# Keys turned two heads at a time, propagators in one stretch, memory rows two blocks a step: a hybrid decoder step on one Trainium2 core

## The chip, the core and the metric

The kernel runs on one core of a Trainium2 chip. The core has a matrix engine (PE; its weight loads are listed apart as PEld), a vector engine (DVE), a scalar engine (ACT), a general engine (POOL) and a queue engine (SP) that mainly issues transfers. Transfers of all queues share sixteen DMA engines. The large memory is HBM; on the core are SBUF (128 partitions) and PSUM, into which PE writes. The metric is the device time of one execution in microseconds, lower is better. Several runs are taken and their median is compared.

## What is computed

One step of a decoder trunk layer: a prompt of 1024 rows of width 1024, and one new row for each of 8 samples with 1024 cached rows. One input projection feeds three groups of heads. Cut to what matters here:

```
h = rms_norm(x, ln_g);  proj = h @ w_in            # 3480 columns, split by group
# 1. NSA: 8 query heads, 2 key heads of 64; compressed, selected and window branches
k_sel = rope(rms_norm(k, k_norm[1]), pos);  k_win = rope(rms_norm(k, k_norm[2]), pos)
ck, cv = compress(rows);  ck = rope(rms_norm(ck, k_norm[0]), cend)
o_nsa = g_c * attend(q, ck, cv) + g_s * attend(q, selected) + g_w * attend(q, window)
# 2. RWKV-7: 4 heads of 64
S <- S diag(w) + (S (-kk)) (kk a)^T + v k^T;   y = S r
# 3. memory: 4 heads of 64 against 256 memory rows
kv = rms_norm(mem, mem_norm_g) @ w_mem_kv;  o_mem = softmax(q k^T / 8) v
cat = concat(o_nsa * silu(z_nsa), o_rw * silu(z_rw), o_mem * silu(z_mem))
y = x + cat @ w_out
```

The reference's scan over rows of the RWKV group is computed in chunks, with propagators that carry the state over a chunk. Single-precision products are made of parts: an operand is split into a high part `hi` and a low part `lo`, and hi·hi, hi·lo and lo·hi are summed in PSUM.

## The kernel before

It has a phase for the projection and all that it feeds (0 to 497 us in the profile), one for attention, and the output projection (from 797 us on).

**Columns.** The projection runs in blocks of 128 columns of `w_in`. `w_load` (line 268) issues a 512 KB transfer of raw weights on SP's queue into a buffer `wraw`. `w_split` (line 277) makes `whi` on ACT (line 282) and `wlo` on DVE (line 283). `project` multiplies with the transposed rows into tiles `p_pr`: three matmuls for each of eight k, over pieces of 256, 264 and 512 rows (line 306). There are two buffers each for `wraw`, `whi` and `wlo`. The memory's key and value weights, in four blocks of two k (`mem_kv`, lines 1142 to 1147), take the same buffers, in turn with the columns. A buffer for a load comes free when its earlier content was split, one for a split when the earlier matmuls that read it are done.

**The RWKV quarters.** `rwkv_prep` and `rwkv_state` do a quarter of the rows each time, four times. They are generators driven by `drive` (line 597): after a piece of such work that yields n, columns are handed out for n times 1.3 us, so that PE has matmuls while DVE and ACT work on the chain. In `rwkv_state` (lines 932 to 956), for a pair `t` of chunks, `p_g` takes 32 small matmuls, from which DVE makes `PT` (line 945) and `GT` (line 947), each in two instructions of 128x128. A yield of 0.9 lies between the first pair and the second; after the second follow the `p_z` matmuls that read `UV`.

**The ahead stage.** Seventeen of 21 such columns are handed out by `drive`. The four last (columns of `z`, which gates the outputs) alternate with work for the attention:

```
            bg = self.ahead()
            late = self.columns(cols[EARLY:])
            for _ in group(late, 8):
                for _ in islice(bg, BG):
                    pass
```

that is, eight column steps, then eight steps (`BG`) of `ahead`, and so on. `ahead` weaves two generators step by step: one goes through `prompt_cmp` and then `mem_kv`, the other through `attn_keys` for eight blocks of 128 keys and then `q_stack(7)`.

- `attn_keys` (line 1231) loads 128 rows of the normed keys `k_d` into `kd`: four heads (two selected, two window) of 64, in two transfers that write every head twice side by side. Four transposes `p_k` (line 1242) turn each doubled head, so that its 64 dimensions stand on partitions 0 to 63 and again on 64 to 127. ACT makes `kh` (line 1244) and DVE `kl` (line 1245) from it, 128x512.
- `prompt_cmp` turns rows of the compressed branch (`p_xt`, `pxt`), takes them through a small network (`p_hid`, line 1090; `p_co`, line 1104), norms and rotates the result on DVE, copies it on POOL (line 1183) and turns it (`p_k`, line 1190) into `ckh` and `ckl`.
- `mem_kv` (line 1124) turns the memory rows: for each of eight k two transposes `p_mT` (line 1134), `mhi` on ACT and `mlo` on DVE (lines 1137, 1138), one yield a k. Then come the four weight blocks with the matmuls `p_mo` (line 1154).
- `q_stack` turns queries of the last block (`p_q`, line 1307).

The first scores `p_s` (line 83) read `kh` and `kl` and open the attention phase. The order of calls gives the work a priority and the claims of buffers an order; a scheduler then sets the order of instructions on each engine, which is fixed in the program. SP issues its transfers in its own order; one that has to wait holds up those behind it.

Of the kernel before, what the change touches and what calls it, by code (L numbers as in the profile page):

```python
# [10 lines left out]
F32 = mybir.dt.float32  # L11
# [3 lines left out]
AF = mybir.ActivationFunctionType  # L15
OP = mybir.AluOpType
# [10 lines left out]
KB = 2  # L27
# [20 lines left out]
def bc(ap, shape):  # L48
    return ap.to_broadcast(shape)
# [64 lines left out]
class Step:  # L114
# [713 lines left out]
    def rwkv_state(self, Q):  # L828

        nc, PE = self.nc, self.pe  # L830
        V, A, G = nc.vector, nc.scalar, nc.gpsimd
        AM, UV, ar, bk, I = self.AM, self.UV, self.ar, self.bk, self.ident
# [5 lines left out]
        for g, o, p, b in blocks:  # L838
            x = AM[o, 2 * p:2 * p + 2, :, b * 32:b * 32 + 32]
            V.tensor_tensor(x, x, bc(self.eye[o, None, None, :], [32, 2, 4, 32]), op=OP.add)  # L840
            V.tensor_tensor(Tt[o].rearrange("p (t h) e -> p t h e", t=2), x, bc(self.pairs[o, None, None, :], [32, 2, 4, 32]),
                            op=OP.mult)
# [21 lines left out]
        for i in range(1, 5):  # L864
            ps = self.pw.tile([128, 8, 32], F32, name="p_iy", tag="w")
# [7 lines left out]
            elif i < 4:  # L873
                t = i - 2
                pr = self.pw.tile([128, 4, 64], F32, name="p_r", tag="w")
                for h in range(4):
                    for p in range(2):
                        o, k = slice(p * 64, p * 64 + 64), slice(64 - p * 64, 128 - p * 64)
# [4 lines left out]
            ps = self.pw.tile([128, 8, 32], F32, name="p_it", tag="w")  # L883
# [18 lines left out]
        lo, up = [blocks[0][1], blocks[2][1]], [blocks[1][1], blocks[3][1]]  # L902
        Ti = self.Ti
        ps = self.pw.tile([128, 8, 32], F32, name="p_iy", tag="w")
# [7 lines left out]
        ps = self.pw.tile([128, 8, 32], F32, name="p_it", tag="w")  # L912
# [6 lines left out]
        W = [None] * 2  # L919
        for t in range(2):  # L920
            px = self.pw.tile([128, 4, 128], F32, name="p_x", tag="w")
            for h in range(4):
                for p in range(2):
                    o = slice(p * 64, p * 64 + 64)
# [3 lines left out]
            for p in range(2):  # L928
                o = slice(p * 64, p * 64 + 64)
                V.tensor_copy(UV[o, 2 * t + p], px[o, :, 64:128])  # L930
        yield 0.6
        GT, PT = [None] * 2, [None] * 2
        half = [slice(p * 64, p * 64 + 64) for p in range(2)]
        for t in range(2):
            GT[t] = self.rs.tile([128, 2, 2, 64], F32, name="GT", tag=f"GT{t}")
            PT[t] = self.rs.tile([128, 2, 2, 64], F32, name="PT", tag=f"PT{t}")
            pgs = [self.pw.tile([128, 4, 64], F32, name="p_g", tag="w") for _ in range(2)]
            for k in range(2):
                for c in range(2):
                    for h in range(2):  # L940
                        for pg, o, p in zip(pgs, half, range(2)):
                            x = AM[o, 2 * p + t, 2 * c + h, 64:128] if k else bkT[t][o, c, p, h * 64:h * 64 + 64]
                            PE.matmul(pg[half[h], 2 * k + c, :], W[t][o, 2 * c + h, :], x, start=True, stop=True)
            for p, pg in enumerate(pgs):
                V.tensor_tensor(PT[t][:, :, p, :], pg[:, 0:2], bc(self.eye2[:, None, :], [128, 2, 64]), op=OP.add)
            for p, pg in enumerate(pgs):
                V.tensor_tensor(GT[t][:, :, p, :], pg[:, 2:4], ar[:, :, t, 1, p, :], op=OP.add)
            if t == 0:
                yield 0.9
        pz = self.pw.tile([128, 4, 2, 64], F32, name="p_z", tag="w")  # L950
        for n in range(4):
            for c in range(2):
                for h in range(2):
                    PE.matmul(pz[half[h], n, c, :], bkT[n // 2][:, c, n % 2, h * 64:h * 64 + 64], UV[:, n, 2 * c + h, :],
                              start=(n == c == 0), stop=False, skip_group_check=True)
        yield 0.9
        pyy = [self.pw.tile([128, 2, 2, 64], F32, name="p_yy", tag="w") for _ in range(2)]
        for t in range(2):
            for c in range(2):
                for h in range(2):  # L960
                    for p in range(2):
                        PE.matmul(pyy[h][half[1 - p], t, c, :], AM[:, 2 * p + t, 2 * c + h, 64:128], UV[:, 2 * t + p, 2 * c + h, :],
                                  start=(t == c == 0), stop=False, skip_group_check=True)
        Zs = [self.Z]
        for n in range(4):
            Zn = self.rc.tile([128, 2, 64], F32, name="Zn", tag="Z", bufs=5)
            for c in range(2):
                for h in range(2):
                    PE.matmul(pz[half[h], n, c, :], PT[n // 2][half[h], c, n % 2, :], Zs[n][half[h], c, :],
                              start=False, stop=True, skip_group_check=True)  # L970
            V.tensor_tensor(Zn[:], pz[:, n], bc(self.gC[:, :, n:n + 1], [128, 2, 64]), op=OP.mult)
            Zs.append(Zn)
            if n < 3:
                yield 0.8
        self.Z = Zs[4]
        for t in range(2):
            for c in range(2):
                for p, h in ((0, 0), (1, 1), (1, 0), (0, 1)):
                    PE.matmul(pyy[h][half[1 - p], t, c, :], GT[t][half[h], c, p, :], Zs[2 * t + p][half[h], c, :],
                              start=False, stop=(c == 1), skip_group_check=True)  # L980
        ys = []
        for t in range(2):
# [142 lines left out]
    def mem_kv(self):  # L1125
        nc, I, O = self.nc, self.I, self.O
        V, A, PE = nc.vector, nc.scalar, nc.tensor
        xs = self.mem_rows
        his = [self.slot(j, [128, 4, 256], F32R, f"mhi{j}") for j in (4, 0)]
        los = [self.slot(j, [128, 4, 256], F32R, f"mlo{j}") for j in (5, 1)]  # L1130
        for k in range(8):
            ps = self.pM.tile([128, 512], F32, name="p_mT", tag="m")
            for t in range(2):
                PE.transpose(ps[:, t * 128:(t + 1) * 128], xs[t][:, k * 128:(k + 1) * 128], self.ident[:])
            g = self.v("mem_norm_g", k)
            hi, lo = his[k // 4][:, k % 4, :], los[k // 4][:, k % 4, :]
            A.activation(hi, ps[:, :256], AF.Copy, scale=g)
            V.scalar_tensor_tensor(lo, ps[:, :256], g, hi.bitcast(F32), op0=OP.mult, op1=OP.subtract)
            yield
        po = [self.pw.tile([128, 512], F32, name="p_mo", tag="w") for t in range(2)]  # L1140
        for k in range(0, 8, 2):
            raw = self.wr.tile([128, 2, 512], F32, name="wraw")
            nc.sync.dma_start(raw[:], I["w_mem_kv"][0, k * 128:(k + 2) * 128, :].rearrange("(k p) c -> p k c", p=128))
            wh = self.wp.tile([128, 2, 512], F32R, name="whi")
            wl = self.wp.tile([128, 2, 512], F32R, name="wlo")
            A.activation(wh[:], raw[:], AF.Copy)
            V.tensor_tensor(wl[:], raw[:], wh[:].bitcast(F32), op=OP.subtract)
            yield
            for j in range(2):
                for t in range(2):  # L1150
                    cs = slice(t * 128, (t + 1) * 128)
                    h, l = his[k // 4][:, (k + j) % 4, cs], los[k // 4][:, (k + j) % 4, cs]
                    for i, (a, w) in enumerate(((h, wh), (h, wl), (l, wh))):
                        PE.matmul(po[t][:], a, w[:, j], start=(k + j == 0 and i == 0), stop=(k + j == 7 and i == 2))
            yield
        dst = O["mem_kv_prompt"]
        for t in range(2):
            d0 = bass.AP(tensor=dst.tensor, offset=dst.offset + t * 128 * 512, ap=[[512, 128], [1, 512]])
            kv = self.slot(2 + t, [128, 8, 64], F32, f"mkv{t}")
            A.activation(kv[:, 4:8].rearrange("p h d -> p (h d)"), po[t][:, 256:512], AF.Copy)  # L1160
            self.norm_rope(po[t][:, 0:256].rearrange("p (t c) -> p t c", t=1), 5, 1, 4, None, out=kv[:, 0:4])
            nc.sync.dma_start(d0, kv[:].rearrange("p h d -> p (h d)"))
            yield
# [67 lines left out]
    def attn_keys(self, i, tag="m"):  # L1231
        nc = self.nc
        A, G = nc.scalar, nc.gpsimd
        kk = self.kt.tile([128, 4, 2, 64], F32, name="kd4", tag="kd4", bufs=KB)
        for s in range(2):
            nc.sync.dma_start(kk[:, :, s, :], self.k_d[i * 128:(i + 1) * 128, :].rearrange("t (j d) -> t j d", d=64))
        if i % 4 == 0:
            nc.sync.dma_start(self.vs[i // 4][:].rearrange("p k b g d -> p k (b g d)"),
                              self.v_d[i * 128:(i + 4) * 128, :].rearrange("(k p) c -> p k c", p=128))
        ps = self.pM.tile([128, 4, 128], F32, name="p_k4", tag=tag)  # L1240
        for j in range(4):
            nc.tensor.transpose(ps[:, j, :], kk[:, j].rearrange("p s d -> p (s d)"), self.ident[:])
        kh, kl = (x[i // 4][:, :, i % 4 * 128:i % 4 * 128 + 128] for x in (self.kh, self.kl))
        A.activation(kh, ps[:], AF.Copy)
        nc.vector.tensor_tensor(kl, ps[:], kh.bitcast(F32), op=OP.subtract)

    def prompt_cmp(self):
        nc, I, O = self.nc, self.I, self.O
# [1267 lines left out]
```

## Time and profile before

| | |
|---|---|
| Runs | 935.43, 937.71, 943.02 us; median 937.71 |
| Profiled execution | 936.7 us, of which the span 934.9 |
| Granted PE clock, mean | 0.998 |
| First scores `p_s` start | 496.62 us |
| PE busy, 425 to 500 us | 70.31 of 75 us |

Times in the profile count from the span's start. A row of groups gives the line, engine, operation and tiles, then the count, the busy time, the mean of one in ns, and the engine's idle time ahead of it with what ended it. In the timeline the columns are start, duration, engine, line and operation, with idle time and its releaser in brackets. Matmuls overlap, so their starts tell more than their durations. A row of a time slice gives each engine's busy time and number of instructions, then the granted clock, the busy share of the DMA engines and GB/s. A row of a tile's view gives the shortest, median and longest duration in ns.

### The profile page before, as it was taken

The page shows a single profiled execution, that of the slowest core. Times are in us where ns is not written, and L with a number is a line of the kernel's source. Part 1 is how long each engine was busy: PE and PEld are TensorE (multiplying, and loading weights), DVE is VectorE, ACT ScalarE, POOL GpSimd, SP SyncE. Part 2 cuts the span into 40 slices and gives each one's busy share as a digit, 9 for nine tenths or more (in the row PEclk, how much of TensorE's full clock was granted, in tenths as well). Part 3 has the DMA queues.
Part 4 walks back from the last instruction along what each step waited for, and adds up shares of the span by engine and source line. Part 5 has one row for each costly group of instructions (what it writes and reads, how often), then busy time and mean ns, then how long its engine had stood idle before and what let it go on. Part 6 is the DMA issues. An engine that isn't in the chain of part 4 may idle for free.

```text
span 934.9 us, 24813 instructions
## 1 busy us (share of the span) xinstructions
PE 899.3 (96%) x9911; PEld 762.7 (82%) x9911; DVE 648.0 (69%) x2013; ACT 434.2 (46%) x987; POOL 178.7 (19%) x270
## 2 busy tenths in 40 slices
PE   8999999999999999999899999999999999999998
PEld 7998888877878788778777788888887887887976
DVE  7668679864777559946457866765678996548454
ACT  7654324232443234213446666666566766424211
POOL 2000000000000000000104444544344765112010
PEclk9999999999999999999999999999999999999999
DMA  8521313241321205524429313432130036986561
GB/s 278 130 78 35 104 41 105 61 115 48 84 86 52 77 19 143 136 65 132 138 85 275 99 56 108 132 108 60 32 87 10 10 113 168 330 249 218 179 239 47
DMA packets 134698, 105.96 MB, mean 113 GB/s; under 512 B 34641, under 2 KB 120600, under 8 KB 134456
## 3 DMA queue, kind: packets, MB, share of 16 engines
q1 hardware_dynamic: 129592, 92.64, 33.8%
q0 software_dynamic: 3200, 10.49, 3.2%
q8 instruction: 78, 1.28, 0.5%
q10 hardware_dynamic: 1792, 1.26, 0.5%
q14 instruction: 36, 0.29, 0.1%
HBM read 85.77 MB, written 22.78 MB: 116 GB/s over the span
## 4 chain that ended last, share of the span: by engine, by line
PE 73%; DVE 17%; ACT 5%; DMA 2%; issue 2%; POOL 0%; SPq 0%; DVEq 0%; ACTq 0%
PE p_pr L86 20%; PE p_out L86 9%; PE p_pr L306 5%; PE p_o L86 5%; PE p_s L86 5%; PE p_pT L86 5%; PE p_hid L86 3%; ACT p L1416 2%; DVE p L1409 2%; PE p_it L86 1%; PE p_iy L86 1%; PE p_sc L86 1%; DVE pt L1377 1%; DVE wlo L283 1%; PE p_tk L86 1%
## 5 line engine op out<-in xcount | busy, mean ns | idle before, releaser
L86 PE MATMUL p_pr<-h,whi 128*128 128x512 f32 (+2 forms) x976 | 237.0, 336 | 2.0 <-DVE zt L318 2.0
L86 PEld LDWEIGHTS p_pr<-h,whi 128*128 128x128 f32 x976 | 158.6, 189 | 19.5 <-issue 2.4
L86 PE MATMUL p_pr<-h,wlo 128*128 128x512 f32 (+2 forms) x488 | 157.6, 326 | 0.6 <-DVE wlo L283 0.6
L1447 POOL TENSOR_SCALAR p<-p,fac,gates 128x640 f32<-128x640 f32 (+7 forms) x128 | 103.3, 817 | 110.9 <-DVE fac L1443 71.1
L1416 ACT ACTIVATE p<-p,nm 128x640 f32<-128x640 f32 (+7 forms) x128 | 93.1, 728 | 56.3 <-DVE nm L1409 51.3
L86 PEld LDWEIGHTS p_pr<-h,wlo 128*128 128x128 f32 x488 | 91.4, 189 | 9.3 <-DVE wlo L283 0.8
L86 PE MATMUL p_pT<-ident,p 128*128 128x128 f32 x528 | 70.8, 279 | 6.9 <-POOL p L1447 1.9
L1075 POOL MEMSET w2d<- 128x128 f32 x1 | 0.2, 204 | 377.2 <-PE p_iy L86 377.2
L86 PEld LDWEIGHTS p_pT<-ident,p 128*128 128x128 f32 x528 | 56.8, 140 | 18.1 <-issue 6.6
L1409 DVE CUSTOM_DVE_ANT_0 p<-p_s,bmask 128x512 f32<-128x512 f32 (+7 forms) x96 | 60.3, 659 | 16.1 <-PE p_s L86 15.4
L306 PE MATMUL p_pr<-h,whi 128*128 128x264 f32 (+2 forms) x320 | 69.3, 310 | 0.0
L86 PE MATMUL p_o<-pt,vs 128*64 128x128 f32 x1056 | 67.9, 276 | 0.4 <-DVE cat L1485 0.4
L283 DVE TENSOR_TENSOR wlo<-wraw,whi 128x1024 fp32r<-128x1024 f32 x33 | 40.3, 1221 | 36.9 <-ACT whi L282 32.6
L86 PE MATMUL p_s<-kh,qs 128*128 128x512 f32 (+3 forms) x191 | 65.2, 354 | 0.2 <-DVE nm L1409 0.2
L282 ACT ACTIVATE whi<-wraw 128x1024 fp32r<-128x1024 f32 x34 | 36.0, 1059 | 59.6 <-PE p_pr L86 47.1
L86 PEld LDWEIGHTS p_o<-pt,vs 128*64 128x64 f32 x1056 | 57.0, 137 | 7.5 <-issue 3.9
L86 PE MATMUL p_s<-kl,qs 128*128 128x512 f32 (+3 forms) x192 | 60.3, 334 | 0.0
L1377 DVE COPY pt<-p_pT 128x512 f32<-128x512 f32 (+1 forms) x72 | 48.2, 673 | 13.2 <-PE p_pT L86 12.4
L306 PEld LDWEIGHTS p_pr<-h,whi 128*128 128x128 f32 x320 | 51.5, 188 | 3.1 <-issue 0.2
L86 PE MATMUL p_out<-woh,chi 128*128 128x512 f32 x128 | 51.7, 404 | 0.0
L86 PE MATMUL p_out<-woh,clo 128*128 128x512 f32 x128 | 50.2, 392 | 0.4 <-DVE clo L2352 0.4
L86 PE MATMUL p_out<-wol,chi 128*128 128x512 f32 x128 | 49.9, 390 | 0.0
(551 smaller groups left out, 1884.3 us busy)
## 6 DMA issues: line engine op xcount, KB each, us to landing
wraw<-in_w_in_dram SPq DMA_DIRECT2D x34, 512.0 KB
pg<-in_c_pool_dram SPq DMA_DIRECT2D x32, 256.0 KB
pg<-in_c_pool_dram SPq DMA_DIRECT2D x48, 128.0 KB
x<-in_x_prompt_dram SPq DMA_DIRECT2D x8, 512.0 KB
z_d<-zt SPq DMA_DIRECT2D x16, 256.0 KB
cat<-z_d SPq DMA_DIRECT2D x8, 512.0 KB
xres<-in_x_prompt_dram POOLq DMA_DIRECT2D x16, 256.0 KB, 3.8
out_dram<-xres POOLq DMA_DIRECT2D x16, 256.0 KB, 3.0
```

Source lines behind the costliest of these rows:

```text
L86: self.last = getattr(self.engine, op)(*a, **k)
L282: nc.scalar.activation(hi[:, :, :n], raw[:, :, :n], AF.Copy)
L283: (low or nc.vector).tensor_tensor(lo[:, :, :n], raw[:, :, :n], hi[:, :, :n].bitcast(F32), op=OP.subtract)
L306: self.last_mm = self.pe.matmul(ps[:m, :b - a], w[:, k, :m], h[k][:, a:b], start=(k == 0 and i == 0), stop=(k == 7 and i == 2))
L1075: nc.gpsimd.memset(w2d[:], 0.0)
L1377: nc.vector.tensor_copy(pt[:, :n], ps[:, :n])
L1409: return V.tensor_tensor_reduce(halves(x), halves(ps), m, -1.0, 3.0e38, op0=OP.add, op1=OP.min, accum_out=nm[:, h, b:b + 1])
L1416: e = A.activation(x, x, AF.Exp, scale=-1.0, bias=nm[:, h, b:b + 1], accum_out=sm[:, h, b:b + 1])
L1447: nc.gpsimd.tensor_scalar(x, x, f[:, h, b:b + 1], gate[:, hd + h, 1 + b:2 + b], op0=OP.mult, op1=OP.mult)
```

## The change

Three edits. Keys: a block is loaded once, 128 rows of 1 KB; a transpose turns two heads at a time, so that heads 0 and 2 land on partitions 0 to 63 and heads 1 and 3 on 64 to 127. ACT and DVE write each half where it belongs in `kh` and `kl` (two instructions of 64x2x128 each). After blocks 3 and 7, four transfers from SBUF to SBUF of 256 KB each fill in the other half. Propagators: `PT` and `GT` of both pairs become one tile each, the `p_g` matmuls of both pairs and `p_z` follow in one stretch, and the two yields of 0.9 become one of 1.6. Memory rows: two k share a PSUM tile and a step, so `mem_kv` has four steps for its transposes instead of eight.

```
-        for t in range(2):
-            GT[t] = self.rs.tile([128, 2, 2, 64], F32, name="GT", tag=f"GT{t}")
-            PT[t] = self.rs.tile([128, 2, 2, 64], F32, name="PT", tag=f"PT{t}")
-            pgs = [self.pw.tile([128, 4, 64], F32, name="p_g", tag="w") for _ in range(2)]
-            for k in range(2):
+        GT = self.rs.tile([128, 2, 2, 2, 64], F32, name="GT", tag="GT")
+        PT = self.rs.tile([128, 2, 2, 2, 64], F32, name="PT", tag="PT")
+        pgs = [self.pw.tile([128, 2, 4, 64], F32, name="p_g", tag="w") for _ in range(2)]
+        for k in range(2):
+            for t in range(2):
                 for c in range(2):
...
-            for p, pg in enumerate(pgs):
-                V.tensor_tensor(PT[t][:, :, p, :], pg[:, 0:2], bc(self.eye2[:, None, :], [128, 2, 64]), op=OP.add)
-            for p, pg in enumerate(pgs):
-                V.tensor_tensor(GT[t][:, :, p, :], pg[:, 2:4], ar[:, :, t, 1, p, :], op=OP.add)
-            if t == 0:
-                yield 0.9
+        for p, pg in enumerate(pgs):
+            V.tensor_tensor(PT[:, :, :, p, :], pg[:, :, 0:2], bc(self.eye2[:, None, None, :], [128, 2, 2, 64]), op=OP.add)
+        for p, pg in enumerate(pgs):
+            V.tensor_tensor(GT[:, :, :, p, :], pg[:, :, 2:4], ar[:, :, :, 1, p, :].rearrange("p c t e -> p t c e"), op=OP.add)
...
-        yield 0.9
+        yield 1.6
...
-        for k in range(8):
-            ps = self.pM.tile([128, 512], F32, name="p_mT", tag="m")
-            for t in range(2):
-                PE.transpose(ps[:, t * 128:(t + 1) * 128], xs[t][:, k * 128:(k + 1) * 128], self.ident[:])
...
+        for k0 in range(0, 8, 2):
+            ps = self.pM.tile([128, 2, 256], F32, name="p_mT", tag="m")
+            for k in (k0, k0 + 1):
+                for t in range(2):
+                    PE.transpose(ps[:, k % 2, t * 128:(t + 1) * 128], xs[t][:, k * 128:(k + 1) * 128], self.ident[:])
...
             yield
...
-        kk = self.kt.tile([128, 4, 2, 64], F32, name="kd4", tag="kd4", bufs=KB)
-        for s in range(2):
-            nc.sync.dma_start(kk[:, :, s, :], self.k_d[i * 128:(i + 1) * 128, :].rearrange("t (j d) -> t j d", d=64))
+        kk = self.kt.tile([128, 2, 128], F32, name="kd4", tag="kd4", bufs=KB)
+        nc.sync.dma_start(kk[:].rearrange("p a b -> p (a b)"), self.k_d[i * 128:(i + 1) * 128, :])
...
-        for j in range(4):
-            nc.tensor.transpose(ps[:, j, :], kk[:, j].rearrange("p s d -> p (s d)"), self.ident[:])
+        for j in range(2):
+            nc.tensor.transpose(ps[:, j, :], kk[:, j], self.ident[:])
...
-        A.activation(kh, ps[:], AF.Copy)
-        nc.vector.tensor_tensor(kl, ps[:], kh.bitcast(F32), op=OP.subtract)
+        half = [slice(0, 64), slice(64, 128)]
+        for g, o in enumerate(half):
+            A.activation(kh[o, g::2], ps[o, 0:2], AF.Copy)
+            nc.vector.tensor_tensor(kl[o, g::2], ps[o, 0:2], kh[o, g::2].bitcast(F32), op=OP.subtract)
+        if i % 4 == 3:
+            for x in (self.kh[i // 4], self.kl[i // 4]):
+                for g in range(2):
+                    nc.sync.dma_start(x[half[1 - g], g::2].bitcast(F32), x[half[g], g::2].bitcast(F32))
```

PE has 16 instructions less (7001 for 7017), DVE 8 less, ACT 8 more; SP's transfers are 559 as before. Three places show what the scheduler makes of it. On PE in the first RWKV quarter, the difference (- before, + after) around the propagators:

```order
 L86 MATMUL p_pr<-h_7_914,whi 128x512
 L86 MATMUL p_pr<-h_7_913,wlo 128x512
-L86 MATMUL p_g<-bkT,W 64x64 x8
-L86 MATMUL p_g<-AM,W 64x64 x8
+L86 MATMUL p_g<-bkT,W 64x64 x16
+L86 MATMUL p_g<-AM,W 64x64 x16
+L86 MATMUL p_z<-UV,bkT 64x64 x16
 L86 MATMUL p_pr<-h_0_245,whi 128x256
```

The second pair's `p_g` and the `p_z` matmuls come forward to the first pair's, and the columns that stood between follow them. On PE in the ahead stage, before, from the compressed branch's output to the memory rows' first transposes:

```order
L1104 MATMUL p_co<-w2d,phid 128x128
L1307 MATMUL p_q<-ident,qhl 128x128 x4
L306 MATMUL p_pr<-h_2_249,whi 128x264
...
L306 MATMUL p_pr<-h_2_811,whi 128x512
L1190 MATMUL p_k<-ident,kd 128x128
L1134 MATMUL p_mT<-ident,mx_6337 128x128
L1134 MATMUL p_mT<-ident,mx_6356 128x128
L306 MATMUL p_pr<-h_2_810,wlo 128x512
```

And after, a little earlier to the same place:

```order
L1240 MATMUL p_k_6524<-ident,kd_6522 128x128 x2
L1279 MATMUL p_xt<-ident,px_6360 128x128 x4
L1240 MATMUL p_k_6539<-ident,kd_6537 128x128 x2
L1087 MATMUL p_hid<-pxt_6483,w1s_6351 128x128 x8
L1311 MATMUL p_q<-ident,qhl 128x128 x4
L1087 MATMUL p_hid<-pxt_6515,w1s_6352 128x128 x8
L1311 MATMUL p_q<-ident,qhl 128x128 x4
L1101 MATMUL p_co<-w2d,phid 128x128
L1311 MATMUL p_q<-ident,qhl 128x128 x4
L1189 MATMUL p_k<-ident,kd 128x128
L1132 MATMUL p_mT<-ident,mx_6305 128x128
```

Before, 26 columns' matmuls stand between `p_co` and the compressed keys' `p_k`, and others further ahead; after, none. On SP's queue, before, the third late column's weights (`wraw` from `w_in`) are asked for right behind the small constants:

```order
L1143 DMA wraw<-in_w_mem_kv_dram 128x2x512
L1040 DMA pe_rows<-in_cmp_pe_dram 32x128
L1067 DMA b1t<-in_cmp_b_dram 64x2x1
L1080 DMA b2b<-in_cmp_b_dram 128x128
L1077 DMA w2d<-in_cmp_w_dram 64x64 x2
L274 DMA wraw<-in_w_in_dram 128x8x128
```

After, the memory's second block stands at that place, and the third column comes behind the eighth key load:

```order
L1234 DMA kd_6490<-k_d 128x256
L1142 DMA wraw<-in_w_mem_kv_dram 128x2x512
L1249 DMA kh_6225<-kh_6225 64x2x512 x2
L1249 DMA kl_6226<-kl_6226 64x2x512 x2
L1234 DMA kd_6506<-k_d 128x256
L1234 DMA kd_6522<-k_d 128x256
L319 DMA z_d<-zt 128x512
L321 DMA z_d<-zt 128x8
L319 DMA z_d<-zt 128x512
L1234 DMA kd_6537<-k_d 128x256
L274 DMA wraw<-in_w_in_dram 128x8x128
```

Here the third memory block and the copies of the first four key blocks also stand ahead of the sixth key load.

More of the change, by code (lines that the diff above doesn't have):

```diff
@@ L931, in rwkv_state @@
         yield 0.6
-        GT, PT = [None] * 2, [None] * 2
         half = [slice(p * 64, p * 64 + 64) for p in range(2)]
-        for t in range(2):
-            GT[t] = self.rs.tile([128, 2, 2, 64], F32, name="GT", tag=f"GT{t}")
-            PT[t] = self.rs.tile([128, 2, 2, 64], F32, name="PT", tag=f"PT{t}")
-            pgs = [self.pw.tile([128, 4, 64], F32, name="p_g", tag="w") for _ in range(2)]
-            for k in range(2):
+        GT = self.rs.tile([128, 2, 2, 2, 64], F32, name="GT", tag="GT")
[3 more added lines that the diff above has]
+            for t in range(2):
                 for c in range(2):
@@ L942, in rwkv_state @@
                             x = AM[o, 2 * p + t, 2 * c + h, 64:128] if k else bkT[t][o, c, p, h * 64:h * 64 + 64]
-                            PE.matmul(pg[half[h], 2 * k + c, :], W[t][o, 2 * c + h, :], x, start=True, stop=True)
-            for p, pg in enumerate(pgs):
-                V.tensor_tensor(PT[t][:, :, p, :], pg[:, 0:2], bc(self.eye2[:, None, :], [128, 2, 64]), op=OP.add)
-            for p, pg in enumerate(pgs):
-                V.tensor_tensor(GT[t][:, :, p, :], pg[:, 2:4], ar[:, :, t, 1, p, :], op=OP.add)
-            if t == 0:
-                yield 0.9
+                            PE.matmul(pg[half[h], t, 2 * k + c, :], W[t][o, 2 * c + h, :], x, start=True, stop=True)
+        for p, pg in enumerate(pgs):
+            V.tensor_tensor(PT[:, :, :, p, :], pg[:, :, 0:2], bc(self.eye2[:, None, None, :], [128, 2, 2, 64]), op=OP.add)
+        for p, pg in enumerate(pgs):
+            V.tensor_tensor(GT[:, :, :, p, :], pg[:, :, 2:4], ar[:, :, :, 1, p, :].rearrange("p c t e -> p t c e"), op=OP.add)
         pz = self.pw.tile([128, 4, 2, 64], F32, name="p_z", tag="w")
@@ L968, in rwkv_state @@
                 for h in range(2):
-                    PE.matmul(pz[half[h], n, c, :], PT[n // 2][half[h], c, n % 2, :], Zs[n][half[h], c, :],
+                    PE.matmul(pz[half[h], n, c, :], PT[half[h], n // 2, c, n % 2, :], Zs[n][half[h], c, :],
                               start=False, stop=True, skip_group_check=True)
@@ L978, in rwkv_state @@
                 for p, h in ((0, 0), (1, 1), (1, 0), (0, 1)):
-                    PE.matmul(pyy[h][half[1 - p], t, c, :], GT[t][half[h], c, p, :], Zs[2 * t + p][half[h], c, :],
+                    PE.matmul(pyy[h][half[1 - p], t, c, :], GT[half[h], t, c, p, :], Zs[2 * t + p][half[h], c, :],
                               start=False, stop=(c == 1), skip_group_check=True)
@@ L1130, in mem_kv @@
         los = [self.slot(j, [128, 4, 256], F32R, f"mlo{j}") for j in (5, 1)]
-        for k in range(8):
-            ps = self.pM.tile([128, 512], F32, name="p_mT", tag="m")
-            for t in range(2):
-                PE.transpose(ps[:, t * 128:(t + 1) * 128], xs[t][:, k * 128:(k + 1) * 128], self.ident[:])
[L1135 to L1138, printed above, removed]
+        for k0 in range(0, 8, 2):
[3 more added lines that the diff above has]
+                    PE.transpose(ps[:, k % 2, t * 128:(t + 1) * 128], xs[t][:, k * 128:(k + 1) * 128], self.ident[:])
+            for k in (k0, k0 + 1):
+                g = self.v("mem_norm_g", k)
+                hi, lo = his[k // 4][:, k % 4, :], los[k // 4][:, k % 4, :]
+                A.activation(hi, ps[:, k % 2], AF.Copy, scale=g)
+                V.scalar_tensor_tensor(lo, ps[:, k % 2], g, hi.bitcast(F32), op0=OP.mult, op1=OP.subtract)
             yield
```

## The prediction, written before the changed kernel ran

> **What bounds the kernel now.** I read the page first: one engine is busy nearly all the time, and the chain that ended last runs mostly through it.
>
> ```profile
> PE 899.3 (96%) x9911; PEld 762.7 (82%) x9911; DVE 648.0 (69%) x2013; ACT 434.2 (46%) x987; POOL 178.7 (19%) x270
> ...
> PE 73%; DVE 17%; ACT 5%; DMA 2%; issue 2%; POOL 0%; SPq 0%; DVEq 0%; ACTq 0%
> ```
>
> So PE's own order sets the time. DVE, ACT and the DMA queue cost only where PE stands still for them. PE takes its instructions strictly in the program's order, so such a standstill can only be filled by matmuls placed at that point of the order. Next I read busy time in slices of 5 us around the key and memory stage. Its last line sums fifteen slices, 425 to 500.
>
> ```profile
> 445.00:450.00 5.00, 3.14 (x20) 2.48 (x18) 0.78 (x2) 2.35 (x4) 0.00 (x0) 1.00 0.56 146
> 450.00:455.00 5.00, 4.38 (x34) 3.75 (x34) 3.06 (x5) 2.70 (x7) 0.00 (x0) 1.00 0.76 189
> 460.00:465.00 5.00, 4.85 (x36) 4.43 (x36) 3.90 (x20) 1.98 (x7) 0.00 (x0) 1.00 0.01 3
> ...
> sum 75.00, PE 70.31 PEld 58.45 DVE 40.50 ACT 28.82 POOL 3.19; mean PE 4.69 PEld 3.90 DVE 2.70 ACT 1.92 POOL 0.21
> ```
>
> PE idles 75.00 - 70.31 = 4.7 us of the 75. The waits of PE in that stretch say for whom:
>
> ```profile
> PE p_k L1242 <- DMA kd<-k_d: 2.4, 2, 1.9
> PE p_mo L1154 <- DVE wlo L1147: 0.5, 1, 0.5
> PE p_k L1190 <- POOL kd L1183: 0.5, 1, 0.5
> ```
>
> Idle time is low because late projection columns (`p_pr`, line 306) stand between the steps of three long chains. The timeline of PE shows it:
>
> ```profile
> 433.85 0.63 PE L1242 MATMUL p_k<-ident,kd 128*128 128x128 f32 x4 [0.59 <-DMA kd<-k_d]
> ...
> 448.44 0.63 PE L1242 MATMUL p_k<-ident,kd 128*128 128x128 f32 x4 [1.86 <-DMA kd<-k_d]
> 448.91 0.60 PE L1275 MATMUL p_xt<-ident,px 128*128 128x128 f32 x4
> ...
> 458.56 0.60 PE L1307 MATMUL p_q<-ident,qhl 128*128 128x128 f32 x4
> 458.91 0.48 PE L306 MATMUL p_pr<-h,whi 128*128 128x256 f32 x2
> ...
> 460.85 0.46 PE L1104 MATMUL p_co<-w2d,phid 128*128 128x128 f32 x2
> 461.14 0.60 PE L1307 MATMUL p_q<-ident,qhl 128*128 128x128 f32 x4
> 461.50 0.49 PE L306 MATMUL p_pr<-h,whi 128*128 128x264 f32 x2
> ...
> 466.31 0.33 PE L1190 MATMUL p_k<-ident,kd 128*128 128x128 f32 x1 [0.49 <-POOL kd L1183]
> ...
> 496.62 0.39 PE L83 MATMUL p_s<-kh,qs 128*128 128x512 f32 x1
> ```
>
> Durations overlap on PE, so I use starts. Four key transposes take 448.91 - 448.44 = 0.47, or 0.117 each. The path from `p_co` to the compressed keys' transpose takes 466.31 - 460.85 = 5.46 us, and PE shows only 0.49 of it as idle: columns fill the rest.
>
> From the first key transpose to the first scores are 62.8 us (433.85 to 496.62). At their start-to-start pitch (0.117 for 128 columns, 0.234 for 512) the instructions there need 53.3 us by my count. The other 9.5 us are 4.1 of idle time (4.7 less the 0.59 ahead of the first row) and 5.4 of handovers: PE goes into a group of transposes and out again about 20 times, 0.27 each.
>
> **Keys, the direct part.** Sixteen transposes go: 16 x 0.117 = -1.9 us, all on PE's path. Each block is now emptied by ACT, DVE, ACT, DVE in turn, on half the partitions but 256 elements each, instead of one ACT and one DVE pass over 512. The nearest rows:
>
> ```profile
> L1244 ACT ACTIVATE kh<-p_k 128x512 fp32r<-128x512 f32 x8 | 4.8, 598 | 10.9 <-PE p_k L1242 10.9
> ...
> L1146 ACT ACTIVATE whi<-wraw 128x1024 fp32r<-128x1024 f32 x4 | 4.2, 1061 | 8.9 <-PE p_pr L306 5.1 <-PE p_mo L1154 3.8
> ...
> L1160 ACT ACTIVATE mkv<-p_mo 128x256 f32<-128x256 f32 x2 | 0.7, 374 | 0.0
> ...
> L1245 DVE TENSOR_TENSOR kl<-p_k,kh 128x512 fp32r<-128x512 f32 x8 | 5.5, 689 | 8.1 <-ACT kh L1244 8.1
> ...
> L382 DVE TENSOR_TENSOR mkv<-p_mo,rq_r 128x256 f32<-128x256 f32 x2 | 0.8, 424 | 0.1
> ```
>
> That is 2 x (0.374 + 0.424) = 1.6 us a block in place of 0.598 + 0.689 = 1.29. With columns between the blocks neither is seen. Where blocks stand next to each other, it is.
>
> **Keys, the transfers.** Sixteen loads become eight, and eight SBUF copies are added, all on SP's queue.
>
> ```profile
> 429.91 1.26 SPq L1236 DMA_DIRECT2D kd<-k_d  x2
> ...
> kd<-k_d SPq DMA_DIRECT2D x16, 128.0 KB
> ```
>
> The issues stay sixteen at about 0.63 us, so SP itself is neither better nor worse off. The first pair was issued by 431.17 and used at 433.85, 2.7 later; one load instead of two may bring it 0.6 earlier, or not at all. I take 0 there. Bytes: 16 x 128 KB become 8 x 128 KB and 8 x 256 KB, one MB more, in a stretch whose DMA engines stand at 0.56 to 0.76. The first four copies (1 MB) and a memory weight block (512 KB) now stand ahead of the sixth and seventh key loads. At the 189 GB/s of the 450 row they take up to 8 us. Most of that passes under fifteen column matmuls (15 x 0.234 = 3.5) and the transposes before. I take 1.2 us of waiting for the sixth load, with bounds 0 and 5. The second four copies land long before 496: 0.
>
> [...] No run here shows such a copy yet.
>
> **Memory rows, and what that moves.** The sixteen transposes, eight ACT and eight DVE passes remain; bundling saves perhaps two handovers. But `mem_kv` yields four times fewer, and steps of `ahead` and column steps alternate in fixed groups. So its first two weight blocks now claim buffers before the third late column, which must wait for the second block's matmuls. The order shows the consequence: the columns that stood between the eighth key block, `p_hid`, `p_co`, the compressed keys and the memory transposes are gone from there, and follow after the memory matmuls. The work is the same, but these chains lose their cover. Chain by chain:
>
> 1. Key blocks six to eight stand back to back with the last two `p_xt`: three emptyings of 1.7 us (1.6 and handoffs) are 5.1, less 14 transposes x 0.117 = 1.6 that run meanwhile: 3.5 us. Lower end 2.0, if ACT runs ahead of DVE; upper end 4.6, if the second weight block's split (1.06 on ACT), queued right ahead of the sixth block's pass, delays that in full.
> 2. Second `p_hid` to `p_co`: 460.85 - 458.56 = 2.29, less one `p_q` of 0.35: 1.9. The first `p_hid` to the second: 0.3.
> 3. `p_co` to the transpose: 5.46, less `p_co` and `p_q` (461.50 - 460.85 = 0.65) and less the column's pass that DVE did in the middle (0.34 between these two starts):
>
> ```profile
> 465.16 0.42 DVE L318 SCALAR_TENSOR_TENSOR zt<-zt,p_pr 128x264 f32<-128x264 f32 x1
> 465.50 0.18 DVE L398 TENSOR_TENSOR nr_o<-nr_o,nr_sq 128x32 f32<-128x32 f32 x1
> ```
>
> That leaves 4.5 us. Nothing else stands there for PE.
> 4. Memory transposes to `p_mo`: 0.5, as the waits of before have for the same matmuls.
>
> New waits: 0.6 for the first load (as before), 1.2, 3.5, 0.3, 1.9, 4.5, 0.5 = 12.5. Handovers: 14 groups in place of 20, 14 x 0.27 = 3.8. Together 16.3 against 4.7 + 5.4 = 10.1 before: +6.2 us.
>
> **Propagators.** Per quarter, both pairs in one stretch: one trip less from columns to 64-wide matmuls and back, and four DVE passes of 256 for eight of 128.
>
> ```profile
> L945 DVE TENSOR_TENSOR PT<-p_g,c_rw x16: 277/282/291, 133.8 to 415.0; 128x128 f32<-128x128 f32 x16
> ...
> 133.87 0.28 PE L86 MATMUL p_pr<-h,wlo 128*128 128x256 f32 x1
> 134.09 0.33 PE L86 MATMUL p_g<-bkT,W 64*64 64x64 f32 x2
> 134.63 0.40 PE L86 MATMUL p_g<-bkT,W 64*64 64x64 f32 x11 [0.22 <-DVE GT L947]
> ...
> 137.74 0.28 PE L86 MATMUL p_pr<-h,wlo 128*128 128x256 f32 x1
> 137.95 1.15 PE L86 MATMUL p_yy<-UV,AM 128*64 128x64 f32 x32
> ```
>
> A trip costs about 0.1 on entry (137.74 to 137.95 is 0.21 where the pitch is 0.117) and as much on leaving: 0.2. The 0.22 wait for `GT` goes once. DVE saves 4 x (2 x 0.28 - 0.424) = 0.5 a quarter, off the path. Sum 4 x 0.2 + 0.2 = -1.0 us. Bounds: -2 (a later wait goes too) to +1.5 (PT and GT of the first pair come later, and a filler step less is handed out).
>
> **Sum.** +6.2 - 1.9 - 1.0 = +3.3 us. After the first scores PE's order is the same, and their inputs do not arrive late, so it is kept to the end. The profiled execution took 936.7 us around its span of 934.9; it lies 1.0 below the median of the runs, 937.71. So 936.7 + 3.3 + 1.0 = 941.0 us.
>
> **Rivals.**
> - *Cover not needed.* Chains shorten where nothing interleaves: load wait 0 (-1.2), key emptying 2.0 (-1.5), handovers counted inside waits (-2.0), propagators at -2 (-1.0). Then 941.0 - 5.7 = 935.3, faster than before. It decides once waits and handovers of the stage stay under 10.1 + 2.9 = 13.0. For it: 5.4 is a remainder, not a row. Against it: items 2 and 3 are durations of chains in the trace, 6.4 us by themselves. Chance 0.20.
> - *The queue.* The copies hold up the sixth to eighth key loads at the upper bound, 5 us: 941.0 + 3.8 = 944.8. For it: the 1.86 wait for a key load at 448.44, behind far less traffic. Chance 0.15.
> - *A cold clock.* A gap of 4.5 us slows PE for a while after. The trace has such a place at the start, after 2.73 us of waiting:
>
> ```profile
> 3.32 5.18 PE L86 MATMUL p_w<-ident 128*128 128x128 f32 x30
> ...
> 10.14 3.62 PE L86 MATMUL p_w<-ident 128*128 128x128 f32 x30
> ```
>
> The same thirty cost 1.6 us more the first time: 941.0 + 1.6 = 942.6. Against it: no wait elsewhere exceeds 2.7, and the clock column reads 1.00 in every slice. Chance 0.10. [...]
>
> **Chances.** The forecast as summed has 0.55; the rivals 0.20, 0.15 and 0.10. From 935.3 to 944.8, widened by a microsecond at either end for the runs' scatter: 934.5 to 946.0. Within 1% (9.4 us, about what a measurement of this kernel can tell from no change) lies nearly all of it: 0.88. Slower by more than that needs the queue and the clock together with the sum, 0.08; faster by more would need the stage's waits gone altogether, 0.04.
>
> **What would show it.** In the profile after: `p_k` of the compressed keys waiting some 4.5 us for POOL or DVE, `p_co` some 2 for DVE, the late key blocks for DVE's `kl`; the first scores at about 500; PE's busy time about 3 us less (1.9 of it transposes). Scores at or before 496.6 would make the forecast wrong; so would key loads that arrive over 3 us after PE is ready for them, or `p_mT` and `p_mo` at half pace.

## The result

The changed kernel took 945.46 us (median of 22 runs, 941.09 to 952.14) against 937.94 for the kernel before (22 runs, 935.43 to 943.02). The ratio is 1.0076, 95% interval 1.006 to 1.0091: by the ratio some 7.1 us slower. The profiled execution took 947.2 us with a span of 945.4, so it is slower than the median run.

| profiled span, us | before | after |
|---|---|---|
| last state matmul `p_yy` of the RWKV quarters starts | 420.6 | 418.9 |
| first scores `p_s` start | 496.6 | 507.4 |
| the stage between | 76.0 | 88.5 |
| from the first scores to the end | 438.3 | 438.0 |

The quarters end 1.7 us earlier, the stage is 12.5 longer, and nothing happens behind it. In the page's view of 40 slices the place is seen at once, in the rows of PE and of its clock:

```profile
PE   8999999999999999898699999999999999999998
...
PEclk9999999999999999999699999999999999999999
```

The 6 in the second row is new: the slice around 460 us. One 5 us slice at a time (the columns as before, the clock right after POOL's count):

```profile
430.00:435.00 5.00, 3.02 (x41) 1.75 (x39) 1.51 (x3) 0.76 (x2) 0.00 (x0) 0.78 0.81 250
435.00:440.00 5.00, 5.00 (x38) 4.98 (x38) 3.58 (x11) 1.69 (x5) 0.00 (x0) 0.88 0.56 168
...
445.00:450.00 5.00, 2.26 (x10) 1.50 (x8) 1.81 (x2) 1.54 (x2) 0.00 (x0) 0.99 0.94 231
450.00:455.00 5.00, 3.37 (x13) 2.20 (x13) 1.79 (x5) 3.01 (x7) 0.72 (x1) 0.50 0.67 190
455.00:460.00 5.00, 5.00 (x23) 4.78 (x24) 1.12 (x3) 1.40 (x5) 0.73 (x1) 0.50 0.52 125
...
465.00:470.00 5.00, 0.76 (x5) 0.75 (x5) 2.98 (x18) 1.31 (x5) 0.41 (x2) 0.69 0.00 0
470.00:475.00 5.00, 5.00 (x22) 4.06 (x21) 2.13 (x5) 2.12 (x6) 0.00 (x0) 0.62 0.00 0
```

Two things go on here: PE waits (2.26, 3.37 and 0.76 us busy out of 5), and three times its clock falls to half: around 434 (0.50 from 434 to 436), from 450 to 460 (0.50), and from 467 to 474 (0.50 from 468 to 472). A slice with a busy PE and a clock of 0.50 looks full and does less: from 455 on, sixteen `p_hid` matmuls take 0.21 us each from start to start, where the kernel before needed 0.12 (rows in the last section). PE's waits of the stage:

```profile
PE p_k L1189 <- POOL kd L1182: 4.2, 1, 4.2
PE p_k L1240 <- DMA kd<-k_d: 2.8, 1, 2.8
PE p_k L1240 <- DMA vs<-v_d: 2.0, 1, 2.0
PE p_co L1101 <- DVE phid L1094: 1.7, 1, 1.7
PE p_k L1240 <- ACT pxt L1281: 1.4, 2, 0.7
PE p_xt L1279 <- DVE kl L1245: 0.2, 1, 0.2
```

They sum to 12.3 us, where the stage before had 4.7. The whole stage in one slice, for the kernel after:

```profile
418.90:507.40 88.50, 76.20 (x455) 64.14 (x449) 44.40 (x158) 30.46 (x71) 3.23 (x6) 0.88 0.43 121
```

and before:

```profile
420.60:496.62 76.02, 71.33 (x468) 59.40 (x463) 41.85 (x149) 29.10 (x63) 3.19 (x6) 1.00 0.44 126
```

PE is busy for 4.9 us more, with 13 matmuls less on record. The clock explains it: summed over 2 us slices, busy time times the missing share of the clock is 8.0 us. This is an estimate, which takes PE to be as slow as its clock; in the trace a `p_mo` matmul of 512 columns took 0.425 us from start to start at 472 us (clock 0.50 to 0.56), one of `p_pr` 0.235 at 445 (clock 1.00), by which it would be an estimated 7.2. With the 8.0, PE's busy time at a full clock would be 76.2 - 8.0 = 68.2, or 3.1 less than before. So in this execution: waits +7.6, work -3.1, clock +8.0, together +12.5; quarters -1.7, the rest -0.3; sum +10.5, as the spans have it (945.4 - 934.9). This is an account of one execution, and its terms are not independent: a slow transpose fills time in which a fast one would leave PE waiting. So a full clock need not have given back all of the 8.0.

The runs agree. Each of the 22 lists its mean granted clock, from 0.982 (952.14 us) to 0.995 (941.09), and a straight line through them falls by 0.7 us for each thousandth, with a correlation of -0.86. Their mean is 0.989. The clocks of the 22 runs of the kernel before are not on record; in the three later comparisons it has 0.996 (31 runs) and 0.995 (26 and 23). By the line through the changed kernel's runs, the difference is worth an estimated 4.3 to 4.7 of the 7.1 us.

### The profile page after: what moved, and what is told of

The parts are those of the page before. It is cut to its first block, busy times and chain, and to the rows that moved or that the text cites. A ratio compares the mean times of both kernels' runs of the same rounds, so it can differ in the third digit from the quotient of the medians.

```text
span 945.4 us, 24777 instructions
## 1 busy us (share of the span) xinstructions
PE 901.8 (95%) x9895; PEld 766.3 (81%) x9895; DVE 648.2 (69%) x2005; ACT 435.4 (46%) x995; POOL 178.6 (19%) x270
## 3 DMA queue, kind: packets, MB, share of 16 engines
q8 instruction: 78, 1.28, 0.5%
## 4 chain that ended last, share of the span: by engine, by line
PE 74%; DVE 15%; ACT 5%; DMA 2%; issue 2%; SPq 1%; POOL 0%; DVEq 0%; ACTq 0%; POOLq 0%
PE p_pr L86 20%; PE p_out L86 9%; PE p_pr L306 7%; PE p_o L86 5%; PE p_s L86 5%; PE p_pT L86 4%; PE p_hid L86 3%; ACT p L1420 3%; DVE p L1413 2%; PE p_it L86 1%; PE p_iy L86 1%; PE p_sc L86 1%; PE p_mo L1153 1%; DVE pt L1381 1%; PE p_tk L86 1%
```

## The experiments

There were three comparisons, each with runs of the kernel before that its kernels share (31, 26 and 23), so ratios are compared, not times. A ratio is not the quotient of the two medians beside it, and can differ from it by 0.0016. The question was first which edit is to blame, then how much is cover and how much the clock.

| run | edit | median, us | before there | ratio, 95% interval | stage, us | PE idle in it |
|---|---|---|---|---|---|---|
| rwkv_alone | propagators only | 935.59 | 936.03 | 1.0001 (0.998 to 1.0022) | 76.6 | 4.8 |
| keys_alone | keys only | 934.69 | 936.03 | 0.9981 (0.9956 to 1.0006) | 74.3 | 4.2 |
| claims_alone | before, four steps fewer | 944.02 | 936.03 | 1.0091 (1.006 to 1.0122) | 83.5 | 10.2 |
| steps_back | after, four steps more | 935.35 | 936.03 | 0.9986 (0.9964 to 1.0008) | 74.3 | 4.2 |
| claims_filled | claims_alone, gap filled | 945.58 | 936.74 | 1.0078 (1.0052 to 1.0103) | 82.3 | 6.5 |
| after_filled | after, gap filled | 943.14 | 936.74 | 1.0073 (1.0044 to 1.0101) | 82.9 | 7.4 |
| copies_elsewhere | after, copies on POOL's queue | 941.84 | 936.74 | 1.0049 (1.003 to 1.0067) | 79.2 | 8.4 |
| six_steps | after, BG = 6 | 930.02 | 936.74 | 0.994 (0.9918 to 0.9961) | 71.0 | 2.2 |
| six_before | before, BG = 6 | 936.93 | 937.75 | 1.0003 (0.9982 to 1.0023) | 73.5 | 3.2 |
| six_no_rwkv | six_steps without propagators | 931.62 | 937.75 | 0.9939 (0.9918 to 0.9961) | 71.0 | 2.5 |
| six_copies_elsewhere | six_steps, copies on POOL's queue | 932.12 | 937.75 | 0.9945 (0.9923 to 0.9966) | 71.9 | 3.1 |

The stage is that of the first table, from one profile each. In all of them the rest behind it is 437.7 to 442.8 us; in the four at 441 and more (keys_alone, claims_filled, copies_elsewhere, six_before) PE was slow there for a while: their longest weight load for `p_s` is 333 or 334 ns, 192 to 195 in the others.

**The propagators alone.** Edit: the hunk of `rwkv_state` on the kernel before.

> The propagator edit alone, on the kernel before. My theory: it gains 1.0 to 1.7 us (the prediction's term was -1.0; the last state matmuls of the changed kernel's profile end 1.7 us earlier than before), so 936.2 to 936.9 against 937.9, clock 0.998, waits of the key stage as before. Rival (the merged stretch makes later steps wait, which eats the gain): 937.9 or more.

The quarters end at 418.8 instead of 420.6, 1.8 earlier, and the first scores come at 495.4 instead of 496.6. Over 12 and 31 runs no gain is left to see: 1.0001, with 0.998 still inside the interval. In the profile 0.6 of the 1.8 comes back in the stage (76.6 instead of 76.0). A reason may be that the shorter yields (1.6 for 1.8) hand out fewer columns in the quarters; no run tests it.

**The keys alone.** Edit: the hunk of `attn_keys` on the kernel before.

> The key edit alone: one load a block, two transposes, copies across partitions; memory rows step as before. My theory: columns still stand in the late chains, so only the 16 transposes count: -1.9 us, 936.0. Rival (the copies on the queue and the longer emptying of a block are what costs): a wait of 2 us or more for a key load stays, and the time is 940 or above.

0.9981 is 1.8 us, the size of the sixteen transposes, though the interval just includes 1. The waits for key loads fall from 2.4 to 1.2 us, all of it at the fourth block, ahead of the copies. Over thirty column matmuls stand between the fifth block and the sixth, and behind the same copies on the same queue PE waits for no key load. So with columns in between, neither the copies nor the longer emptying show as a loss.

**The steps alone.** All instructions of the kernel before, with one line changed:

```
             V.scalar_tensor_tensor(lo, ps[:, :256], g, hi.bitcast(F32), op0=OP.mult, op1=OP.subtract)
-            yield
+            if k % 2:
+                yield
```

> The kernel before with one edit: the memory rows' transposes yield after every second k only, all instructions as before. My theory (fewer steps shift the buffer claims, the third late column comes after the memory matmuls, the chains lose their cover, and PE's clock falls in the gaps): 944 to 947, granted clock below 0.995, PE waits over 4 us for POOL at the compressed keys' transpose. Rival (the loss comes from the keys' transfers): 938 as before.

This is as much as the whole loss: 1.0091, with an interval that holds 1.0076. No key, no propagator and no bundle of memory rows is changed; only where the generator gives way. The waits for the compressed keys and for `p_co` are those of the changed kernel; those for the first and the sixth key load are not there:

```profile
PE p_k L1191 <- POOL kd L1184: 4.3, 1, 4.3
PE p_co L1104 <- DVE phid L1097: 1.7, 1, 1.7
PE p_k L1243 <- ACT pxt L1278: 1.2, 2, 0.7
PE p_k L1243 <- ACT whi L1147: 1.1, 1, 1.1
```

The order of the matmuls shows the reason that the prediction gave: the third late column is claimed behind the memory's second block, so no column stands in the three chains.

**The steps restored.** The reverse, on the changed kernel:

```
                 V.scalar_tensor_tensor(lo, ps[:, k % 2], g, hi.bitcast(F32), op0=OP.mult, op1=OP.subtract)
             yield
+            yield
```

> The changed kernel with one edit: after each pair of memory blocks two yields instead of one, so that there are eight steps again. My theory: claims and cover as before, no clock loss; what remains are the gains, -1.9 and -1.0 to -1.7: 934.3 to 935.0. Rival (the keys' transfers and emptying cost by themselves): 940 or above, with the waits for a key load still there.

One empty yield takes back the loss: 0.9986 against 1.0076. Idle time is 4.2 us, where the kernel before has 4.7. The 2.9 to 3.6 us of gain that I expected do not show: the ratio gives 1.3, though the lower end of its interval, 0.9964, would be 3.4.

**The gap filled.** Behind `p_co`, 32 transposes of the identity, one after the other:

```
+        warm = self.pw.tile([128, 512], F32, name="p_w", tag="w")
+        last = self.co
+        for _ in range(32):
+            with self.tc.issue_after(last.ins):
+                last = PE.transpose(warm[:, :128], self.ident[:], self.ident[:])
```

> The kernel of claims_alone with 32 transposes that nobody reads put behind p_co, into the 4.3 us in which PE waits for the compressed keys. It does 3.7 us more work on PE. Theory A (the idle gap itself costs about 5.4 us of cover, and the lower clock after it the other 2.6 of the 8.0): the clock stays at 1.00 behind the gap, and the kernel comes to about 5.4 above before. Theory B (only the missing cover costs, the clock drop hits work that waits anyway): 8 above before, or more.

At the place itself theory A holds. Without the filling the clock falls in the gap (0.68 from 460 to 462 us, 0.50 from there to 470), and what follows is slow (timeline of claims_alone, PE):

```profile
464.57 0.48 PE L1191 MATMUL p_k<-ident,kd 128*128 128x128 f32 x1 [4.25 <-POOL kd L1184]
464.84 0.64 PE L1134 MATMUL p_mT<-ident,mx 128*128 128x128 f32 x2
...
470.93 0.41 PE L1134 MATMUL p_mT<-ident,mx 128*128 128x128 f32 x2
```

With it (claims_filled) the clock reads 1.00 in every slice of 2 us from 462 to 472:

```profile
467.20 0.33 PE L1191 MATMUL p_k<-ident,kd 128*128 128x128 f32 x1 [0.76 <-POOL kd L1184]
467.36 0.38 PE L1134 MATMUL p_mT<-ident,mx 128*128 128x128 f32 x2
...
471.27 0.44 PE L1134 MATMUL p_mT<-ident,mx 128*128 128x128 f32 x2
```

From the compressed keys' transpose to the sixth pair of memory transposes it takes 4.07 us instead of 6.36, and `p_co` to that transpose is no longer than before (5.14 and 5.15 us). So the drop behind this gap costs 2.3 us. The two runs also bear out what the prediction says of PE's order: in claims_alone PE stands for 4.25 us ahead of `p_k`, with the memory transposes behind it in the order; here the 32 transposes ahead of it run from 462.35 on, and 0.76 of the wait is left. The total did not follow: 1.0078 against 1.0091, intervals that overlap. In this profile PE was slow elsewhere: at 453 us over the last key block and `p_hid` (four transposes in 1.12 us, sixteen matmuls in 2.97, against 0.66 and 1.98 in claims_alone), and in the attention phase, where the page's clock reads 8 tenths from 710 to 734 us. The runs' mean clock is 0.994, hardly above the 0.992 of claims_alone.

> The changed kernel with the same 32 unread transposes behind p_co. Here the clock falls three times (at 432, 450 and 468 us); this fills only the last gap. Theory A: the half clock over the memory transposes and the first p_mo goes, about 2 us: 5 above before instead of 7.1; the two earlier drops stay. Theory B: no change, 7 above before.

Here too the wait for the compressed keys is down to 0.8 us. But the waits for key loads are others too: none is longer than 1.5 us, where the changed kernel has one of 2.8 and one of 2.0. The page's clock reads 8 tenths from 447 to 470 us, 6 from 449 to 473 in the changed kernel. So the first scores at 502.5 instead of 507.4 in the profile can't be put down to the filled gap alone. The ratio, 1.0073 from six runs, can't be told from 1.0076. What one drop is worth to the total is left open by both runs; that a lower mean clock comes with more time is shown by the runs' own clocks (0.7 us for each thousandth in the changed kernel's).

**The copies on another queue.** Edit: `nc.gpsimd.dma_start` for the eight copies.

> The changed kernel with the eight copies issued from POOL's queue instead of SP's; the scheduler then spreads the column matmuls between the last key blocks, claims unchanged. Theory A (the copies ahead of the sixth key load cost its wait of 2.8 us and, by the clock drop behind that wait, about as much again): 2 to 4 above before. Theory B (the load is late because the DMA engines are full, whoever issues): the wait of 2 us or more stays, 6 to 7 above before.

The time is 4.6 above before, between the two theories, and the interval (2.8 to 6.3) reaches into both. The wait of 2.8 us for the sixth load falls to 0.8 for all key loads, and the first scores come at 497.5, ten us earlier than in the changed kernel's profile. Its stage is only 3.2 us longer than before; this profile ends 442.8 behind the first scores instead of 438.3, with the page's clock at 8 tenths from 705 to 729 us, in the attention phase. And the scheduler also spread the columns otherwise, so the copies' place and the cover of the key blocks are not told apart here. The wait of 4.3 for the compressed keys remains, since the claims are as in the changed kernel, and the page's clock reads 8 tenths from 447 to 470 us, around it.

**Six steps.** Edit: `BG = 6` in the changed kernel.

> The changed kernel with six steps of ahead instead of eight between two groups of column steps (BG = 6). The third late column is then claimed ahead of the first memory block, and columns stand in all three chains. Theory: the chains are covered, no clock drop in this stage, the gains remain: 1 to 3 below before. Rival (the new steps do not fit six either): above before.

It beats both: 0.994, or 5.6 us below the kernel before, and more than the 1 to 3 expected. The waits of the stage are nearly gone, and the stage is 71.0 us long:

```profile
PE p_k L1189 <- POOL kd L1182: 0.7, 1, 0.7
PE p_k L1240 <- DMA kd<-k_d: 0.7, 2, 0.5
PE p_mo L1153 <- ACT mhi L1136: 0.6, 1, 0.6
...
417.60:488.60 71.00, 68.83 (x458) 58.63 (x450) 43.69 (x158) 30.35 (x71) 3.24 (x6) 1.00 0.50 145
```

PE is busy for 68.8 us at a clock of 1.00, close to the estimated 68.2 that the changed kernel would have had at one.

> The kernel before with BG = 6 and nothing else. Control for six_steps. If the gain of six_steps comes from the step count alone, this stands 5 to 6.7 below before too. If the three edits are worth their 3 to 4 us (16 transposes 1.9, propagators 1.0 to 1.7), this stands 2 to 3 below before, and six_steps below it by the rest.

The control shows that the step count alone gives nothing in total: with six steps the kernel before stays as it was, 1.0003. In its profile the stage is 2.5 us shorter all the same, and the part behind it 3.1 longer (441.4 for 438.3, with weight loads for `p_s` of up to 333 ns, 194 in the kernel before). So the edits and the six steps together are worth 5 to 6 us. The six steps without the edits, and the edits with their eight steps back, bring nothing clear of noise. My split was wrong here: I gave the step count 2 to 3 us of its own.

> six_steps without the propagator edit (key and memory edits, BG = 6). If the propagators in one stretch are worth the 1.0 of the prediction, this stands about 1 above six_steps, that is 0.993 to 0.996 of before; if they are worth nothing (as rwkv_alone has it, 1.0001), at the same time as six_steps.

0.9939: the same as six_steps with 0.994. The propagators bring nothing that these runs can show; the gain is that of the keys and the memory rows with six steps. The two were not taken apart.

> six_steps with the copies issued from POOL's queue. With columns in all chains the copies' place on SP's queue should not matter: within 1 us of six_steps. Rival (the copies still hold up key loads or weights on SP): 1 to 3 below six_steps.

0.9945, as six_steps. With columns in every chain no effect of the copies' place on the queue is seen.

## Why the prediction came out as it did

The direction, the place and the loss of cover were right: 941.0 was forecast, the range reached 946.0, and 945.46 was measured. The sum was not, by one term. One of the prediction's own signs of being wrong came in the profiled execution, `p_mT` at little more than half pace (eight in 1.67 us from start to start, 0.21 each for the 0.117 of the prediction's transposes; clock 0.50 to 0.56 from 468 to 474 us), and the first scores came at 507.4, not at about 500. That 945.46 still lies inside the range is partly luck. The upper end was the price of the queue rival, 944.8, and a microsecond for scatter, and the loss came mostly by another way. Without the estimated 8.0 of the clock the profile has +2.5, near the +3.3 of the sum.

- *The waits.* 12.5 us were forecast and 12.3 measured, item by item: the compressed keys 4.5 and 4.2, `p_co` 1.9 and 1.7, the sixth load 1.2 and 2.8, the first 0.6 and 2.0, the emptying of key blocks 3.5 and 1.6. The last three miss one by one and cancel, and the two small items, 0.3 and 0.5, do not show. Of the 1.9 that the emptying fell short, the half clock may have taken a part: the 14 transposes that run meanwhile, 1.6 at full pace, ran slower there (four `p_xt` in 1.06 and 1.11 us at 450 and 453, 0.66 at 443). The first load came late although it was asked for 1.6 us earlier (428.28 for 429.91), since PE was ready for it earlier still (430.61 for 433.26); PE's wait names the `vs` transfer, issued next to it, that of the weight load names `kd` (2.2).
- *The work.* PE's busy time in the stage is an estimated 3.1 us less at a full clock, where the sum had 3.5 (transposes 1.9, handovers 1.6).
- *The propagators.* -1.0 was forecast; the quarters end 1.7 earlier, but the runs of the edit alone show 1.0001. Between -1.9 and +2.1 us, the interval of that run, it stays open.
- *The clock.* This is the step that failed. "A cold clock" was a rival with a chance of 0.10 and a price of 1.6 us, for one drop behind the longest gap. The lower clock came, three times in this stage of the profiled execution, and is worth an estimated 4.3 to 4.7 us over the runs. The argument against it was wrong: "no wait elsewhere exceeds 2.7, and the clock column reads 1.00 in every slice". The first half is true and does not help, since at 432 the clock fell behind a wait of 1.98. As to the second, the column reads 1.00 in the slices around the key stage, not over the whole span. In slices of 50 us the kernel before has one row below 1.00, which the prediction left out of account:

```profile
250.00:300.00 50.00, 48.04 (x377) 41.37 (x376) 33.63 (x101) 19.55 (x38) 0.00 (x0) 0.97 0.24 70
```

Finer slices show what is in it, a drop behind a wait of 2.0 us:

```profile
274.00:276.00 2.00, 0.76 (x3) 0.67 (x4) 2.00 (x9) 0.00 (x0) 0.00 (x0) 1.00 0.24 76
276.00:278.00 2.00, 2.00 (x7) 1.54 (x6) 0.27 (x1) 0.00 (x0) 0.00 (x0) 0.61 0.89 319
278.00:280.00 2.00, 2.00 (x7) 1.55 (x6) 0.00 (x0) 0.00 (x0) 0.00 (x0) 0.53 0.00 0
```

With forecast waits of 4.5, 3.5 and 1.9 us close together, these rows would have given the drop more than 0.10. They would not have given its size: this one costs an estimated 1.7 us (two busy slices at 0.61 and 0.53), as the rival had it, and a wait of 1.86 us at 448 in the same trace has no drop behind it (1.00 in each slice of 2 us from 448 to 456). In hindsight, 941.0 with 4.3 to 4.7 more gives 945.3 to 945.7.

- *The other rivals.* "Cover not needed" fell: the chains' latencies stood in the waits nearly in full. "The queue" took part, with 2.8 us at the sixth load of the 5 it allowed, and alone it does not decide: keys_alone has the same copies and is no slower. How the 2.8 divide between the copies and the missing columns stays open.

## What to carry to other kernels

Where generators are interleaved by counting steps, a change in the number of yields is a change of the schedule: the claims on shared buffers move, and with them the work that covers the chains. When bundling makes steps fewer, set the ratio of steps anew, and look at the order of instructions before any run; here one empty yield decided some 8 us (1.0076 against 0.9986), and `BG = 6` turned a loss of 7 us into a gain of 5.6. Price a new idle gap on PE twice, once for the gap and once for a lower clock behind it (4.25 and 2.3 us in claims_alone), and look for the clock in fine slices over the whole span first.

## What was not expected of the hardware

PE's clock fell to about half behind waits of 1.96 us (before, at 275 us: 0.53 from 278 to 280), 1.98 (after, at 432: 0.50 from 434 to 436) and 2.82 (after, at 450: 0.50 in every slice of 2 us from there to 460). It fell behind a shorter one too: 1.28 us (after, at 319: 0.54 from 320 to 322). Behind 1.86 us (before, at 448) it stayed at 1.00. So the length of the wait alone does not decide, and which wait is long enough is not shown. The drop at 450 held for 10 us:

```profile
455.43 3.62 PE L1087 MATMUL p_hid<-pxt,w1s 128*128 128x128 f32 x16
458.85 1.05 PE L1311 MATMUL p_q<-ident,qhl 128*128 128x128 f32 x4
```

The sixteen matmuls of `p_hid` take 3.42 us from start to start, where the kernel before, at a clock of 1.00, needed 1.97:

```profile
453.98 1.98 PE L1090 MATMUL p_hid<-pxt,w1s 128*128 128x128 f32 x16
455.95 0.66 PE L1307 MATMUL p_q<-ident,qhl 128*128 128x128 f32 x4
```

The clock column does not show every slow stretch: at the very start (2 to 8 us) it reads 1.00, while thirty transposes took 5.18 us, 1.6 longer than the 3.62 of thirty others a little later, as the prediction quotes.
